# A graph attention layer on one core: block 0's bins taken inside the last merge, block 1's spread by TensorE, the sort ended at stretches of four

## The chip, the cores and the metric

The kernel runs on one core of a Trainium2 chip. The metric is device time in microseconds (us). Engines are named as the profile names them: PE is TensorE (PEld its weight loads), DVE is VectorE, ACT is ScalarE, POOL is GpSimd, and SP is the engine that only issues DMAs. PSUM is the memory that PE writes and DVE and ACT read; a line such as L514 is a line of the kernel before.

## What is computed

A graph has 4096 nodes with 64 features and 50,000 directed edges, drawn at random. For each of 4 heads, the features are projected to 64 outputs, each edge gets a score from its two ends, and each node receives the mean of its sources' projections, weighted by the exponentials of the scores:

```python
x_proj[h] = x @ weight[h]
...
src_att = np.sum(x_proj[h, src_nodes] * att_src[h], axis=-1)
dst_att = np.sum(x_proj[h, dst_nodes] * att_dst[h], axis=-1)
...
edge_scores = np.where(edge_scores > 0, edge_scores, 0.2 * edge_scores)
...
output[h, dst] += np.exp(edge_scores[h, i]) * x_proj[h, src]
...
output[h, dst] /= (total + 1e-8)
```

The output is 4096 x 256 in float32.

## The kernel before

The edges have to be brought to their nodes first, and this is done by sorting.

**First sort (to 68 us).** Each of the 128 partitions holds 391 edges as numeric keys. `Sorter` is a bitonic sorting network on DVE: a step (`half(j)`, L203 to L210) compares elements 2^j apart with one minimum and one maximum. `rows` sorts each partition's row of 512; `runs` (L240) then merges eight rows into a run, in two rounds: transpose, a few steps across rows, transpose back, and the steps j = 8 down to 0 inside the rows. The runs go to memory (`gat_sorted1`). Beside it ACT counts with Sign and an accumulator how many keys of each row lie below each of 17 bounds (`below`, L265), PE adds the counts up (L282), and DVE works out where each group of 256 source nodes begins and ends in each run (`bounds`, L277 to L291: one conversion, then multiply, reduce, add for the starts `ws` and again for the ends `we`).

**Second sort (72 to 115 us).** POOL gathers, for each of 16 source groups, its share of each run (`fetch`, L308). Eight partitions make one source group now. They are merged the same way, this time by destination, and the last step writes the keys as integers (`ki`), which SP stores to memory (`gat_sorted2`, L263). ACT counts again, against 33 bounds, one for each block of 125 destination nodes, and the same `bounds` gives the start of each block in each group.

**The seam (115 to 131 us).** `Windows` (L377) has POOL gather, in 5 pieces of 8 blocks each, the 128 keys from each start on: 16 rows of 128 keys for a block, enough for all of its edges and some of its neighbours'. `unpack(i)` (L386) splits a piece into the source within the group and the destination within the block (`tb`, two halves) with four small operations on DVE, or three on DVE and one on ACT for piece 0, and stores both to memory (`gat_bins`). `Blocks.load(b)` (L414) reads them back so that every partition has all 2 x 2048 numbers of block b (`bc`, 1 MB written). For block 0 alone this is done without memory: `spread` (L421) has PE multiply `tb` with one column of the identity repeated 128 times, once per row, and ACT and DVE copy the result from PSUM. Between them stand two `longest` (L293), which find the longest stretch of the first and of the second sort (two small DVE operations, a transpose by PE, and a maximum into `most`); `room` (L303) has every engine read `most` into registers, for a test at the end of the kernel: if a stretch is longer than its window (256 and 128), a second, general pass runs. Six dense matmuls whose result nobody reads follow on PE (`warm`, L646).

**The blocks (131 to 297 us).** `Blocks.run` (L520) takes the 33 blocks in order. For a block: `onehot` (L436) compares `bc` with the partition's number and leaves 0/1 matrices `oh` (DVE, two instructions, L446 and L449); `gather(b, c)` (L452) has PE multiply them with the node tables, in three parts of 6, 6 and 4 groups, each part into one of two PSUM buffers, and ACT takes the exponentials (`ex`, L475) and copies the values (`xs`, L477); `weights` (L481) and `values` (L490) make `wv` and `val` on DVE; `sums` (L500) adds the weights up (k < 0) and the values (k = 0 and 1, L514) by PE into `acc`, which ACT copies away (`aT`, L564); `project` (L566) multiplies with the weights, and once for every two blocks `invert` and `give` (L571 to L582) divide and store.

**What sets the order.** Everything up to the test at the end stands in a stretch with a manual schedule: each engine runs its instructions in the order in which the program writes them, and waits only for data and buffers. Block b's iteration issues: `load(b+4)`, `values(b)`, `gather(b+1, 0)`, `project(b-1)`, `sums(b, -1)`, the rest of `gather(b+1)`, the first half of `onehot(b+2)`, `weights(b+1)`, the second half, `sums(b, 0)` and `(b, 1)`. An `unpack` that is handed to `run` (`also`, L545) comes last in its iteration. DMAs are issued in program order too; nearly all are SP's. `bc` has 4 buffers; `oh`, `ex`, `xs`, `wv` and `val` have 2.

Before the change, the seam is written so (L638 to L655):

```python
group(so2, pp2, ws1[:])
win = Windows(cst, ws2[:])
longest(so2, pp2, ws1, we1, 0)
longest(so2, pp2, ws2, we2, 1)
n1, n2 = room(0, EL), room(1, L)
...
win.unpack(0, nc.sync, nc.scalar)
for b in range(1, 4):
    blocks.load(b)
for i in range(1, 4):
    win.unpack(i, nc.sync, nc.sync)
blocks.spread(0, win.tb[:, 0])
blocks.run({i - 3: lambda i=i: win.unpack(i, nc.sync, nc.sync) for i in range(4, NI)})
```

Of the kernel before, what the change touches and what calls it, by code (L numbers as in the profile page):

```python
# [11 lines left out]
P = 128  # L12
ALPHA = 0.2
F32 = mybir.dt.float32
BF16 = mybir.dt.bfloat16
# [6 lines left out]
L = 512  # L22
# [5 lines left out]
BD = 125  # L28
KPAD = float(1 << 24)
# [8 lines left out]
def kernel(ctx: ExitStack, tc: tile.TileContext, x: bass.AP, edge_index: bass.AP,  # L38
# [141 lines left out]
    class Sorter:  # L180
# [59 lines left out]
        def runs(self, to=None):  # L240


            s, d = self.step()
            V.stream_shuffle(out=self.z[:], in_=s[:], mask=[p ^ 1 for p in range(32)])
            V.tensor_scalar(out=self.y[:], in0=s[:], scalar1=sig[:, 0:1], scalar2=None, op0=OP.mult)
            V.scalar_tensor_tensor(out=d[:], in0=av(self.z[:], L - 1, [-1, L]), scalar=sig[:, 0:1], in1=self.y[:],
                                   op0=OP.mult, op1=OP.min)
            s, d = self.step()
            V.tensor_scalar(out=d[:], in0=s[:], scalar1=sj[0][:, 0:1], scalar2=None, op0=OP.mult)
            for j in range(8, -1, -1):  # L250
                self.half(j)
            for m in range(1, 3):
                self.turn()
                self.opposed(m)
                for j in range(m - 1, -1, -1):
                    self.half(j)
                self.turn()
                for j in range(8, -1, -1):
                    self.half(j, to=to if m == 2 and j == 0 else None)
            return to or self.a[self.cur]  # L260
# [16 lines left out]
    def bounds(pool, pp, sgn, nt, n, sels, off, mask, nk, ws, we):  # L277

        ni = ws.shape[1] // len(sels)
        for i, sel in enumerate(sels):  # L280
            ps = pp.tile([P, nt + 1], F32, name=f"cnt_ps{i}")
            T.matmul(out=ps[:], lhsT=sel, rhs=sgn[:], start=True, stop=True)  # L282
            cnt = pool.tile([P, nt + 1], F32, name=f"cnt{i}")
# [9 lines left out]
    def longest(pool, pp, ws, we, k):  # L293

        mx = pool.tile([P, ws.shape[1]], F32, name=f"mx{k}")
        V.tensor_tensor(out=mx[:], in0=we[:], in1=ws[:], op=OP.subtract)
        mx1 = pool.tile([P, 1], F32, name=f"mxr{k}")
        V.tensor_reduce(out=mx1[:], in_=mx[:], axis=AX, op=OP.max)
        mx_ps = pp.tile([1, P], F32, name=f"mx_ps{k}")
        T.transpose(out=mx_ps[:], in_=mx1[:], identity=ident[:])  # L300
        V.tensor_reduce(out=most[:, k:k + 1], in_=mx_ps[:], axis=AX, op=OP.max)
# [15 lines left out]
    def group(pool, pp, start):  # L317
# [7 lines left out]
        so.rows(9)  # L325
        ki = pool.tile([P, L], I32, name="ki")
        store(skey2, so.runs(ki))
        bounds(pool, pp, sgn, 8 * NI, L, [sel2[:]], off2, m8, 8, ws2, we2)
# [73 lines left out]
    class Blocks:  # L402
# [18 lines left out]
        def spread(self, b, tb):  # L421

            bc = self.bc[b] = self.bcp.tile([P, 2, NT * W2], BF16, name="bc")
            for c, (t0, n) in enumerate(CH):
                ps = self.psx.tile([P, CH[0][1], PW], F32, name="ps")
                for i in range(n):
                    T.matmul(out=ps[:, i, :], lhsT=av(identb[:], b * NT + t0 + i, [0, P]), rhs=tb, start=(i % 2 == 0),
                             stop=True, skip_group_check=True)
                (S.copy if c < 2 else V.tensor_copy)(out=av(bc[:], t0 * W2, [W2, n], [NT * W2, 2], [1, W2]),
                                                     in_=av(ps[:], 0, [PW, n], [W2, 2], [1, W2]))  # L430
                if c == 1:
                    self.onehot(b, *CH[0])
            for c in (1, 2):
                self.onehot(b, *CH[c])
# [85 lines left out]
        def run(self, also={}):  # L520
# [4 lines left out]
            for b in range(ND):  # L525
# [89 lines left out]
    with tc.tile_pool(name="sort1", bufs=1) as so1, tc.tile_pool(name="pre", bufs=1) as pr, \  # L615
# [19 lines left out]
        so.rows(1, EL)  # L635
        store(skey1, so.runs())
        bounds(so1, pp1, sgn, NR, EL, [sel1[:, 0, :], sel1[:, 1, :]], off1, m16, NR, ws1, we1)
    with tc.tile_pool(name="sort2", bufs=1) as so2, tc.tile_pool(name="pp2", bufs=1, space=PSUM) as pp2:  # L638
        group(so2, pp2, ws1[:])
        win = Windows(cst, ws2[:])  # L640
        longest(so2, pp2, ws1, we1, 0)
        longest(so2, pp2, ws2, we2, 1)
        n1, n2 = room(0, EL), room(1, L)
        warm = pp2.tile([P, L], F32, name="warm")
        for i in range(6):
            T.matmul(out=warm[:], lhsT=identb[:], rhs=adb[:, 0:4, 0:P], start=True, stop=True)  # L646
    with ExitStack() as st:
        blocks = Blocks(st, Finish(st))
        win.unpack(0, nc.sync, nc.scalar)
        for b in range(1, 4):  # L650
            blocks.load(b)
        for i in range(1, 4):
            win.unpack(i, nc.sync, nc.sync)
        blocks.spread(0, win.tb[:, 0])
        blocks.run({i - 3: lambda i=i: win.unpack(i, nc.sync, nc.sync) for i in range(4, NI)})  # L655
# [3 lines left out]
    with tc.If((n1 > W1) | (n2 > W2)):  # L659
        with tc.tile_pool(name="all", bufs=1) as al:  # L660
            total = al.tile([P, ND, AW], F32)
            V.memset(total[:], 0.0)
            with tc.For_i(0, n1, W1):
                at1 = advance(al, ws1, we1, W1, 1)
                with tc.tile_pool(name="sort3", bufs=1) as so3, tc.tile_pool(name="pp3", bufs=1, space=PSUM) as pp3:
                    group(so3, pp3, at1[:])
                    longest(so3, pp3, ws2, we2, 1)
                m2 = room(1, L)
                with tc.For_i(0, m2, W2):
                    with ExitStack() as st:  # L670
# [6 lines left out]
                        blocks.onehot(0)  # L677
                        blocks.run()
# [40 lines left out]
```

## Time and profile before

| | |
|---|---|
| seven runs | median 300.23 us, 299.18 to 303.67 |
| the profiled execution | 299.06 us, of which the span from first to last instruction is 297.2 |
| busy: PE, DVE, ACT | 200.5 us (67%), 261.2 us (88%), 181.5 us (61%) |
| granted PE clock, mean | 0.855 |
| first sort's store issued | 68.17 |
| second sort's store issued | 114.85 |
| end of the waits for ACT's counts on PE | 105.80 |
| 136 to 284 us | PE busy 146.02 of 148.00, DVE 140.69, ACT 116.02 |

The page of a profile gives, among other things, the busy share of each engine in 40 equal slices (one digit a slice, in tenths; 9 is 90% or more), with the clock that TensorE was granted in the row PEclk. The timeline gives instructions with start and duration in us from the start of the span, and, in brackets, how long the engine sat idle before and what it was waiting for. The waits give, for each pair of waiting and releasing instruction, the us in total, how often, and the longest. Starts of one engine's instructions can lie closer together than their durations, since they overlap in its pipeline; what an instruction costs its engine is then read from start to start.

### The profile page before, as it was taken

Reading aid. Unit: us, or ns where it says so; the run is one execution under the profiler, and the core shown is the slowest. Engines: PE = TensorE matmul, PEld = TensorE weight load, DVE = VectorE, ACT = ScalarE, POOL = GpSimd, SP = SyncE. Lnnn points to the kernel's source line nnn. Section 1 sums busy time; section 2 is a strip of 40 time slices with the busy share of each in tenths; the row PEclk is TensorE's granted clock in tenths of the full one; section 3 lists DMA queues with packets and bytes.
Section 4 is the critical chain, followed back from the end, with each engine's and each line's share of the span. In section 5 each row is a group of like instructions: output and inputs, shape, how many; then the busy total and the mean of one; then the engine's idle time right before and its main releaser. Section 6 shows DMA issues by size and latency. Waiting matters only on the chain.

```text
span 297.2 us, 8429 instructions
## 1 busy us (share of the span) xinstructions
PE 200.5 (67%) x3531; PEld 191.1 (64%) x3531; DVE 261.2 (88%) x495; ACT 181.5 (61%) x355; POOL 27.2 (9%) x78
## 2 busy tenths in 40 slices
PE   0001999950000001769999999999999999999990
PEld 0000699950000000459999999999999999999980
DVE  5999999994699997689999999999999999999960
ACT  2950710050699920477787778777787878777840
POOL 7882000002000001500000000000000000000000
PEclk9999975555555555799999999999999999999997
DMA  3025000001000000497678666875587567854012
GB/s 108 1 57 103 0 2 0 0 1 42 30 0 0 0 0 35 110 385 295 202 273 295 213 206 249 303 249 204 216 306 267 197 210 292 286 195 187 10 39 59
DMA packets 13358, 41.80 MB, mean 141 GB/s; under 512 B 3120, under 2 KB 8816, under 8 KB 9216
## 3 DMA queue, kind: packets, MB, share of 16 engines
q1 hardware_dynamic: 10776, 38.97, 36.2%
q10 hardware_dynamic: 1832, 1.55, 2.2%
q0 software_dynamic: 704, 0.66, 1.1%
q8 instruction: 30, 0.49, 0.7%
q14 instruction: 16, 0.13, 0.1%
HBM read 36.13 MB, written 5.05 MB: 139 GB/s over the span
## 4 chain that ended last, share of the span: by engine, by line
PE 54%; DVE 36%; DMA 4%; issue 3%; POOL 0%; ACT 0%; DVEq 0%; POOLq 0%; SPq 0%
PE acc L514 20%; DVE sA L209 13%; DVE sB L209 12%; PE ps L469 10%; PE pf L568 7%; PE ps L467 6%; PE ps L473 5%; PE acc L509 5%; DMA bc<-gat_bins 2%; DVE sB L238 1%; DMA eS<-in_edge_index_dram 1%; DMA raw<-gat_sorted,wi 1%; PE warm L646 1%; DVE sA L198 1%; DVE val L495 1%
## 5 line engine op out<-in xcount | busy, mean ns | idle before, releaser
L477 ACT CAST xs<-ps 128x1200 bf16<-128x1200 f32 (+1 forms) x99 | 104.1, 1051 | 0.0
L495 DVE TENSOR_TENSOR val<-xs,wv 128x4096 bf16<-128x4096 bf16 (+1 forms) x34 | 75.4, 2221 | 0.6 <-ACT xs L477 0.5
L514 PE MATMUL acc<-xs,val 128*128 128x125 bf16 x1056 | 63.6, 218 | 0.2
L469 PE MATMUL ps<-adb,oh 128*128 128x136 bf16 x528 | 61.4, 223 | 0.0
L467 PE MATMUL ps<-xa,oh 128*128 128x72 bf16 x528 | 58.8, 196 | 3.4 <-DVE oh L446 2.5
L514 PEld LDWEIGHTS <-val 128*128 128x128 bf16 x1056 | 58.8, 98 | 0.5 <-DVE val L495 0.4
L469 PEld LDWEIGHTS <-oh 128*128 128x128 bf16 x528 | 49.0, 98 | 0.4 <-issue 0.3
L467 PEld LDWEIGHTS <-oh 128*128 128x128 bf16 x528 | 46.9, 98 | 3.5 <-DVE oh L446 3.5
L475 ACT ACTIVATE ex<-ps 128x96 bf16<-128x96 f32 (+1 forms) x99 | 25.0, 252 | 31.2 <-PE ps L473 31.2
L446 DVE TENSOR_SCALAR oh<-bc,pF 128x4096 bf16<-128x4096 bf16 (+2 forms) x35 | 42.0, 1201 | 0.8 <-DMA bc<-gat_bins 0.8
L209 DVE TENSOR_TENSOR sA<-sB 128x256 f32<-128x256 f32 (+2 forms) x106 | 38.0, 400 | 1.8
L209 DVE TENSOR_TENSOR sB<-sA 128x256 f32<-128x256 f32 (+2 forms) x100 | 35.9, 400 | 1.7
L473 PE MATMUL ps<-xa,oh 128*128 128x72 bf16 x528 | 33.3, 198 | 0.0
L282 PE MATMUL cnt_ps<-sgn,sel 128*128 128x17 f32 (+1 forms) x6 | 1.7, 390 | 42.1 <-ACT sgn L274 42.1
L282 PEld LDWEIGHTS cnt_ps<-sgn,sel 128*128 128x128 f32 x6 | 1.4, 318 | 42.2 <-issue 42.2
L473 PEld LDWEIGHTS <-oh 128*128 128x128 bf16 x528 | 26.3, 99 | 0.1
L367 PEld LDWEIGHTS at_ps<-uv,xT 64*128 64x128 f32 x130 | 25.2, 302 | 0.2 <-issue 0.2
L367 PE MATMUL at_ps<-uv,xT 64*128 64x4 f32 x130 | 25.3, 331 | 0.0
L449 DVE TENSOR_SCALAR oh<-bc,pF 128x2048 bf16<-128x2048 bf16 (+2 forms) x35 | 25.1, 717 | 0.0
L568 PE MATMUL pf<-Wbd,aT 128*128 128x128 f32 x132 | 22.7, 295 | 2.9 <-ACT aT L564 0.9
L271 ACT ACTIVATE junk<-kr,nb 128x512 f32<-128x512 f32 x33 | 23.8, 722 | 1.1
L568 PEld LDWEIGHTS pf<-Wbd,aT 128*128 128x128 f32 x132 | 17.3, 191 | 4.7 <-issue 3.4
(130 smaller groups left out, 203.2 us busy)
## 6 DMA issues: line engine op xcount, KB each, us to landing
bc<-gat_bins SPq DMA_DIRECT2D x32, 1024.0 KB, 9.0
out_dram<-res SPq DMA_DIRECT2D x32, 125.0 KB
eS<-in_edge_index_dram SPq DMA_DIRECT2D x2, 195.0 KB
eD<-in_edge_index_dram ACTq DMA_DIRECT2D x2, 195.0 KB
gat_bins<-tb SPq DMA_DIRECT2D x9, 32.0 KB
gat_sorted<-sA SPq DMA_DIRECT2D x1, 256.0 KB
gat_sorted<-ki SPq DMA_DIRECT2D x1, 256.0 KB
out_dram<-res SPq DMA_DIRECT2D x1, 96.0 KB
```

The costliest lines, as they stand in the source:

```text
L209: V.tensor_tensor(out=av(d[:], o, [2 * h, n], [1, h]), in0=av(s[:], 0, [2 * h, n], [1, h]), in1=av(s[:], h, [2 * h, n], [1, h]), op=op)
L367: T.matmul(out=ps[:, b, :], lhsT=xT[:, b * step:b * step + P], rhs=uv[:, k, :], start=(b == 0), stop=True, skip_group_check=True)
L446: V.tensor_scalar(out=oh[:, 0:2, e], in0=bc[:, :, e], scalar1=pF[:, 0:1], scalar2=None, op0=OP.is_equal)
L449: V.tensor_scalar(out=oh[:, 2, e], in0=bc[:, 1, e], scalar1=pF[:, 1:2], scalar2=None, op0=OP.is_equal)
L467: T.matmul(out=ps[:, i, P:P + XC], lhsT=oh[:, 1, e], rhs=xa[:, 2 * t, :], start=(i % 2 == 0), stop=False, skip_group_check=True)
L469: T.matmul(out=ps[:, i, 0:S0], lhsT=oh[:, 0, e], rhs=adb[:, b, :], start=False, stop=False, skip_group_check=True)
L473: T.matmul(out=ps[:, i, P:P + XC], lhsT=oh[:, 2, t * W2:(t + 1) * W2], rhs=xa[:, 2 * t + 1, :], start=False, stop=True, skip_group_check=True)
L475: S.activation(out=av(ex[:], 2 * t0, [2, n], [2 * NT, 2 * H], [1, 2]), in_=av(ps[:], P, [PW, n], [1, 2 * H], [0, 2]), func=ACTF.Exp)
L477: S.copy(out=xs[:, t0:t0 + n, 0:P + XC], in_=ps[:, 0:n, 0:P + XC])
L495: V.tensor_tensor(out=av(val[:], h * Dout, [Dout, n], [C, NT], [1, Din]), in0=av(xs[:], S0, [0, n], [XW, NT], [1, Din]), in1=av(wv[:], h * ...
L514: T.matmul(out=self.acc[:, k * BD:(k + 1) * BD], lhsT=val[:, t, k * P:(k + 1) * P], rhs=xs[:, t, 0:BD], start=False, stop=(t == NT - 1), s ...
L568: T.matmul(out=self.pf[:, b % 2, k * P:(k + 1) * P], lhsT=self.aT[:, b % 2, k * BD:k * BD + P], rhs=Wbd[:, k, :], start=(b % 2 == 0 and k ...
```

## The change

- **The sort's end.** In the second sort, the last merge stops after the step j = 2 (`FINE = 2`): the keys then stand in stretches of four, each stretch right as a whole and its four in any order. That step writes `ki` now. The starts `ws2` are rounded down and the ends `we2` up to multiples of four (`whole`, three operations each), so that a window still takes in all of a block's keys.
- **Block 0's bins.** After the merge's step j = 7 the first 128 keys of a group already stand in the first 128 columns of its first row. There a hook, `spy`, makes them relative to the group on DVE (`kb0`), and one step later splits them (`t0`); ACT casts them (`tb0`), and PE spreads them over the partitions, row 8t for group t, with the copies from PSUM all on ACT. Block 0 no longer needs the store, the gather or `unpack(0)`.
- **Block 1.** It is spread by PE from `unpack(0)`'s `tb`, as block 0 was; loads from memory begin with block 2. Its copies are two on ACT and one on DVE.
- **Order.** The one-hots and the gather of block 0 come right after the bounds. `unpack(0)` follows them, with both stores on SP, then the loads of blocks 2 to 4, `weights(0)`, `values(0)`, the spread of block 1, and block 0's sums between the parts of block 1's gather. `unpack(1)`, the two `longest` (with one maximum for both) and the reading of `most` into registers stand before `sums(0, 1)`. `unpack` 2, 3 and 4 stand in the iterations of blocks 1, 2 and 3.
- **The rest.** The six `warm` matmuls are gone. The counting matmul (`counts`) is issued before the merge instead of after it, and its PSUM buffer and that of `longest` are lent by the block stage, whose buffers now exist during the second sort.

```diff
-        def runs(self, to=None):
+        def runs(self, to=None, fine=0, spy=None):
...
-                for j in range(8, -1, -1):
-                    self.half(j, to=to if m == 2 and j == 0 else None)
+                last = fine if m == 2 else 0
+                todo = []
+                for j in range(8, last - 1, -1):
+                    self.half(j, to=to if m == 2 and j == last else None)
+                    if todo:
+                        todo.pop(0)()
+                    if m == 2 and 1 << j == W2 and spy:
+                        todo = spy(self.a[self.cur])
...
+    def whole(pool, t, up, what):
+        i = pool.tile([P, NI], I32, name=f"whole{what}")
+        V.tensor_scalar(out=i[:], in0=t[:], scalar1=float(up), scalar2=None, op0=OP.add)
+        V.tensor_scalar(out=i[:], in0=i[:], scalar1=FINE, scalar2=FINE, op0=OP.logical_shift_right,
+                        op1=OP.logical_shift_left)
+        V.tensor_copy(out=t[:], in_=i[:])
...
-        store(skey2, so.runs(ki))
-        bounds(pool, pp, sgn, 8 * NI, L, [sel2[:]], off2, m8, 8, ws2, we2)
+        cps = counts(pool, pp, sgn, 8 * NI, [sel2[:]])
+        store(skey2, so.runs(ki, FINE, spy))
+        bounds(pool, cps, 8 * NI, L, off2, m8, 8, ws2, we2)
+        whole(pool, ws2, 0, 0)
...
-        def spread(self, b, tb):
+        def spread(self, b, c, tb, row, copy):
+            if c == 0:
+                self.bc[b] = self.bcp.tile([P, 2, NT * W2], BF16, name="bc")
+            t0, n = CH[c]
+            ps = self.psx.tile([P, CH[0][1], PW], F32, name="ps")
+            for i in range(n):
+                T.matmul(out=ps[:, i, :], lhsT=av(identb[:], row(t0 + i), [0, P]), rhs=tb, start=(i % 2 == 0),
+                         stop=True, skip_group_check=True)
+            copy(out=av(self.bc[b][:], t0 * W2, [W2, n], [NT * W2, 2], [1, W2]),
+                 in_=av(ps[:], 0, [PW, n], [W2, 2], [1, W2]))
...
+        def spy(keys):
+            def relative():
+                V.tensor_scalar(out=kb0[:], in0=keys[:, 0:W2], scalar1=goff[:, 0:1], scalar2=None, op0=OP.add)
+            def split():
+                V.tensor_scalar(out=t0[:, 0, :], in0=kb0[:], scalar1=8, scalar2=None, op0=OP.logical_shift_right)
+                V.tensor_scalar(out=t0[:, 1, :], in0=kb0[:], scalar1=SG - 1, scalar2=None, op0=OP.bitwise_and)
+                S.copy(out=tb0[:], in_=t0[:])
+                for c in range(len(CH)):
+                    blocks.spread(0, c, tb0[:], lambda t: RUN * t, S.copy)
+            relative()
+            return [split]
+        group(so2, Lent(), ws1[:], spy)
         win = Windows(cst, ws2[:])
-        longest(so2, pp2, ws1, we1, 0)
-        longest(so2, pp2, ws2, we2, 1)
+        whole(so2, we2, (1 << FINE) - 1, 1)
+        for c in range(len(CH)):
+            blocks.onehot(0, *CH[c])
+            blocks.gather(0, c)
+        win.unpack(0, nc.sync, nc.sync)
+        for b in range(2, 5):
+            blocks.load(b)
+        blocks.weights(0)
+        blocks.values(0)
+        for c in range(len(CH)):
+            blocks.spread(1, c, win.tb[:, 0], lambda t: NT + t, S.copy if c < 2 else V.tensor_copy)
+            if c == 1:
+                blocks.onehot(1, *CH[0])
+        for c in (1, 2):
+            blocks.onehot(1, *CH[c])
+        blocks.sums(0, -1)
+        blocks.gather(1, 0)
+        blocks.sums(0, 0)
+        blocks.gather(1, 1)
+        blocks.gather(1, 2)
+        win.unpack(1, nc.sync, nc.sync)
+        longest(so2, Lent(), (ws1, we1), (ws2, we2))
         n1, n2 = room(0, EL), room(1, L)
-        warm = pp2.tile([P, L], F32, name="warm")
-        for i in range(6):
-            T.matmul(out=warm[:], lhsT=identb[:], rhs=adb[:, 0:4, 0:P], start=True, stop=True)
...
-        blocks.spread(0, win.tb[:, 0])
-        blocks.run({i - 3: lambda i=i: win.unpack(i, nc.sync, nc.sync) for i in range(4, NI)})
+        blocks.sums(0, 1)
+        blocks.weights(1)
+        blocks.onehot(2)
+        blocks.run(1, {i - 1: lambda i=i: win.unpack(i, nc.sync, nc.sync) for i in range(2, NI)})
```

## The prediction

> **What bounds the kernel now.** I read the page's slices first, then the timeline of the stretch where the second sort hands over to the blocks, and last the waits inside the block loop.
>
> ```profile
> PE   0001999950000001769999999999999999999990
> DVE  5999999994699997689999999999999999999960
> PEclk9999975555555555799999999999999999999997
> ```
>
> Each digit is 7.43 us. VectorE (DVE) is full up to slice 15: the two sorts, which end at 114.7. From slice 18 on (133.7) TensorE (PE) is full. Between them lies a seam of some 16 us in which no engine is full, and TensorE enters it at half clock. The change works on this seam. Its timeline (start, duration, engine, line, operation; in brackets the idle time before and what ended it):
>
> ```profile
> 113.89 0.76 DVE L209 TENSOR_TENSOR ki<-sB 128x256 int32<-128x256 f32 x2
> ...
> 115.89 0.16 DVE L312 CAST wi<-ws 128x5 int32<-128x5 f32 x1
> ...
> 117.58 0.94 POOL L314 DMA_INDIRECT win<-gat_sorted,wi  x1 [42.76 <-DVE mxr L298]
> ...
> 120.17 0.23 DVE L388 TENSOR_SCALAR t<-win 128x128 int32<-128x128 int32 x1 [2.12 <-DMA win<-gat_sorted,wi]
> ...
> 123.28 1.28 SPq L417 DMA_DIRECT2D bc<-gat_bins  x3
> ...
> 128.90 1.29 DVE L446 TENSOR_SCALAR oh<-bc,pF 128x4096 bf16<-128x4096 bf16 x1 [0.77 <-DMA bc<-gat_bins]
> ...
> 131.08 2.29 DVE L495 TENSOR_TENSOR val<-xs,wv 128x4096 bf16<-128x4096 bf16 x1
> ```
>
> The sorted keys go to memory (issued 114.85), the windows come back from 117.58 on, the bins go out and block 1's come back at 128.87. The first `val` (block 0) starts at 131.08. After that, the waits of 136 to 284 us show TensorE waiting for almost nothing, and DVE for little:
>
> ```profile
> ACT ex L475 <- PE ps L473: 28.7, 62, 0.7
> DVE wv L487 <- ACT ex L475: 5.6, 15, 0.6
> PEld pf L568 <- issue: 3.4, 15, 0.2
> ...
> PEld L514 <- DVE val L495: 0.2, 1, 0.2
> ```
>
> A pair of blocks takes 9.72 us (152.91 to 162.62), and DVE's `val` ends only 0.1 to 0.5 us before TensorE's sums (L514) want it: 143.0 against 143.07, 147.87 against 148.03, 152.28 against 152.74. So the end moves by what the seam saves, less what DVE is given to do in the loop beyond 0.37 us a pair (5.6 / 15).
>
> **The change, part by part.** I lay the new order of each engine end to end with the durations above; DVE's clock starts from `half(7)` of the last merge, 108.32 as before.
>
> *Sort end.* Steps of the merge start 0.80 apart (112.30, 113.09, 113.89); two fall away: -1.59. Three operations on 128 columns come in (`kb0`, two for `t0`); L388 and L389 stand 0.13 to 0.14 apart: +0.42 taken, 0.3 to 1.1 as ends (1.1 if each costs L392's 0.28 to 0.50). The counts start at about 113.5 instead of 114.57.
>
> *Rounding.* The bounds take 1.32 to the place of `wi`, as now (114.57 to 115.89). Each `whole` adds three dependent operations on 128x5; dependent small ones stand 0.20 to 0.24 apart (114.80, 115.03, 115.27). With `wi` I take 1.25, ends 0.9 and 1.45. Block 0's first one-hot can start at 113.5 + 1.32 + 1.25 = 116.1; before it was 124.53.
>
> *Block 0's bins under the sort.* ScalarE (ACT) has been idle since 105.7. Cast 0.4 (0.30 for half as much); 16 matmuls of 256 columns at half clock 0.213 each (the warm-up's 512 columns stood 0.43 apart); copies 1.34 apart, the last 1.05. The three parts of `bc` are there at 113.7, 115.1 and 116.0; DVE wants them at 116.1, 117.0 and 117.8. Hidden by the end of the sort, with 1.8 us to spare; beyond that each us late is a us on the path.
>
> *gather(0).* TensorE starts 0.65 after the one-hot, 116.75. A part takes 0.75 (the last 0.5) at full clock. At half clock, 1.4, 1.4 and 0.95; ACT behind it (ex and xs 1.2 a part) is done at 122.1, and `val(0)` starts at **122.2**, 8.9 earlier than 131.08. At full clock it is 121.1.
>
> *Block 1 spread by TensorE: here most of that is given back.* The window lands at 119.1 (the store is issued 1.1 earlier, and 2.6 us lie from gather to landing) and DVE splits it by 119.7, but the cast of `tb` (L391, on ACT) is queued behind the six ACT instructions of gather(0): it ends at 122.4. The 16 matmuls, the second store to `gat_bins` and all loads behind it on SP wait for it. ACT copies to 124.6 and 125.8. DVE, the one that ends last, has in its queue: `val(0)` 2.2, to 124.4; one-hot 0.86 from 124.7; copy 1.13 (125.39 to 126.52); one-hots 0.86 and 0.71, to 128.2; `unpack(1)` 0.62, to 128.85; the four small operations of `longest` 0.46; transpose and maximum 0.4 and 0.6, to 130.3. Then it must read `most` into registers:
>
> ```profile
> L305 PEldq TENSOR_LOAD <-most x2: 311/402/492, 117.4 to 118.1; - x2
> L305 DVEq TENSOR_LOAD <-most x2: 321/434/548, 117.8 to 118.4; - x2
> ```
>
> Before, this lay under the wait for the window. Now `weights(1)` and `onehot(2)` are queued behind it on DVE, and `sums(0,1)` and gather(2) on TensorE. From `most` (118.06) to the end of DVE's second load (118.4 + 0.32) it is 0.66: free at 130.95. (For comparison only: the Trainium skill, "DMA: Bandwidth & Descriptors", section "Latency and other measured facts", gives one such load a floor of about 0.6 us. These loads took 0.32 and 0.55, so the row decides; two at 0.6 would take about half a us off the saving.) Then `wv` 0.14, and `onehot(2)` starts at 131.1, gather(2) at 132.4 (before: 135.20), `val(1)` at 132.9 (135.28), the sums of block 1 at 135.5 (138.15): **2.65 earlier**.
>
> Block 2's bins: last store issued at 122.45, loads 2.18 later (121.10 to 123.28), first landing 5.59 after that: 130.2, under DVE's 131.1 by 0.9.
>
> *In the loop.* `unpack` 2, 3 and 4 now stand in iterations 1, 2 and 3, where before only 4 stood, in iteration 1. That is 2 x 0.6 = 1.2 us more on DVE (140.13 to 140.73), `val` being behind it. DVE's waits for `ex` (0.37 a pair) and its lead of 0.46 at block 4 take up about half; 0.65 comes through. Block 4's sums: 150.7 instead of 152.74.
>
> **Sum: 2.65 - 0.65 = 2.0 us earlier.** Against the profiled execution, 299.06 (span 297.2 and 1.86 around it), that is 297.1. The seven times have the median 300.23, so I forecast **298.2**.
>
> **What the clock does** is the largest unknown. The six warm-up matmuls are gone. In the trace TensorE fell to half clock at 40.7 while its row was 100% busy with 4-column matmuls, and came back at 122.26 (0.74 in the stretch 122.0 to 122.5), 3.8 us after the first warm-up matmul. Counted 3.8 us from gather(0)'s start, the clock is back at 120.5: that is the case above. Back already through the 16 spread matmuls (by 116.7), the sum gives 3.1; back only during block 1 (121 to 128), 1.1 to 1.3.
>
> The Trainium skill, "TensorE: Matmul & The Clock Gate", section "What's actually happening", has a rule against deleting the warm-up: the gate counts free-running windows of 3.4 us, a busy one frees the clock, an idle one takes it. The trace's 3.8 us fits one such window. By the rule the spread's 3.6 us can fill a window only if it begins just right, which points to the middle case and not to 3.1.
>
> **Rivals.**
> (A) *The spread warms TensorE*, 3.1 us: 297.1. For it, 16 dense matmuls in 3.6 us; against it, the gap for the PSUM copy and 2.1 idle us after.
> (B) *The clock is late*, back in block 1, 1.2 us: 299.0. For it, gather(0) at half clock waits for ACT's buffers.
> (C) *Block 2's bins come late.* The page's median from issue to landing of a `bc` load is 9.0; then they land at 133.6, 2.5 after DVE wants them, and the time is 300.7: no change. Against it, the first of three loads landed in 5.59. It costs from 6.5 on.
> (D) *Slower: the clock stays at half into the loop.* Its place is gather(1) to the sums of block 2; TensorE needs twice its 4.9 us a block. Laid out so, the saving is 0 with the clock back at 130, and at 136 the kernel is 1.2 slower: 301.4, with 0.3 more for each further us. For it, 40.7 shows that a busy row is not enough; against it, these very matmuls hold the clock at 1.00 from 122.5 on with 50% gaps.
> (E) *The change spoils the windows*: rounding widens them, and one over 128 keys would send the kernel into its second pass, as much again as 71 to 297. Counted on the reference's draw, the widest is 124: not taken.
>
> **Chances.** Forecast 0.39, A 0.22, B 0.18, C 0.10, D 0.10, E 0.01. A measurement of this kernel can tell about 0.3%, 0.9 us, from no change. The forecast's own bounds (1.0 below, 0.8 above by the ends of the small costs) leave it mostly faster, B partly, C on the line, D slower: faster 0.69, within 0.18, slower 0.13. The range: A with the low ends gives 296.3; upward it takes in B and C and leaves out D: 300.7.
>
> **What would show it.** Right: the first `val` near 122; `cast tb` waiting behind `xs` on ACT; gather(2) near 132.4; DVE idle about 1 us around the register loads; TensorE waiting for `val` in iterations 2 and 3; clock at 1.00 from about 120.5. Wrong: `val(0)` later than 123.5 (small operations dearer), `onehot(2)` released by the DMA (C), half clock after 126 (D), or `unpack` without effect on block 4's sums (then 0.6 more is saved).

## The result and the profile after

The changed kernel takes **298.38 us** (median of 31 runs, 296.85 to 301.38); the kernel before took 300.2 (73 runs, 298.77 to 303.95). The ratio is 0.9938, with a 95% interval of 0.9922 to 0.9954: 1.8 us by the medians, where 2.0 were forecast.

The profiled execution of the changed kernel took 300.25 us (span 298.3), 1.9 more than its median; that of the kernel before took 299.06, 1.1 less than its median. Side by side, these two would show a loss, so the first thing to learn is how far one execution stands from the median. The slices of the changed kernel, from its page:

```profile
PE   0001999950000027769999999999999999999980
DVE  5999999994799998678999999999999999999950
PEclk9999975555555555588999999999999999999996
```

A slice is 7.46 us now. Counted from 0, TensorE does more in slices 14 and 15 (the spread and block 0's gather have come forward), yet the row of the clock comes back from 5 one slice later, and only to 8. The timeline of the seam (start, duration, engine, line, operation; in brackets the idle time before and what ended it):

```profile
112.47 0.76 DVE L210 TENSOR_TENSOR ki<-sB 128x256 int32<-128x256 f32 x2
...
116.15 1.08 POOL L340 DMA_INDIRECT win<-gat_sorted,wi  x1 [41.31 <-DVE we L316]
...
118.79 0.23 DVE L416 TENSOR_SCALAR t<-win 128x128 int32<-128x128 int32 x1 [0.69 <-DMA win<-gat_sorted,wi]
...
121.34 0.33 ACT L419 CAST tb<-t 128x128 bf16<-128x128 int32 x1
...
121.51 2.29 DVE L520 TENSOR_TENSOR val<-xs,wv 128x4096 bf16<-128x4096 bf16 x1 [0.49 <-ACT xs L502]
121.72 2.72 PE L456 MATMUL ps<-tb,identb 128*128 128x256 bf16 x12 [1.35 <-ACT tb L419]
...
124.72 0.62 DVE L471 TENSOR_SCALAR oh<-bc,pF 128x1536 bf16<-128x1536 bf16 x1 [0.92 <-ACT bc L458]
...
131.80 0.23 DVE L512 TENSOR_TENSOR wv<-ex 128x128 bf16<-128x128 bf16 x1 [1.37 <-ACT xs L502]
...
133.80 2.29 DVE L520 TENSOR_TENSOR val<-xs,wv 128x4096 bf16<-128x4096 bf16 x1
```

The order is the one laid out: the first `val` 9.6 us earlier than 131.08, the cast of `tb` on ACT behind block 0's `xs`, TensorE waiting for it, DVE waiting 0.92 for the copy. Then almost everything is given back: the second `val` comes at 133.80, against 135.28. In the loop, over the same 136 to 284 us as before, the waits stay small, and TensorE now waits a little for `val` (twice, 0.6 us in all):

```profile
ACT ex L500 <- PE ps L498: 28.8, 61, 0.9
DVE wv L512 <- ACT ex L500: 5.9, 14, 1.3
...
PEld L539 <- DVE val L520: 0.6, 2, 0.5
```

The new wait of the change stands ahead of the loop, in the waits of the whole execution. It is TensorE's stop of 1.8 us at the register loads, ahead of `sums(0, 1)`:

```profile
PE acc L539 <- issue: 1.8, 1, 1.8
```

### The profile page after: what moved, and what is told of

Read it like the earlier page. It is cut to its first block, busy times and chain, and to the rows that moved or that the text cites. A ratio compares the mean times of both kernels' runs of the same rounds, so it can differ in the third digit from the quotient of the medians.

```text
span 298.3 us, 8448 instructions
## 1 busy us (share of the span) xinstructions
PE 205.7 (69%) x3541; PEld 196.3 (66%) x3541; DVE 260.9 (87%) x503; ACT 185.7 (62%) x359; POOL 27.5 (9%) x78
## 4 chain that ended last, share of the span: by engine, by line
PE 50%; DVE 39%; issue 3%; DMA 2%; ACT 2%; DVEq 0%; POOL 0%; POOLq 0%; ACTq 0%
PE acc L539 18%; DVE sA L210 13%; DVE sB L210 12%; PE ps L494 10%; PE pf L595 6%; PE ps L492 6%; PE ps L498 5%; PE acc L534 4%; DVE val L520 2%; DVE sB L239 1%; DVE oh L471 1%; DMA eS<-in_edge_index_dram 1%; ACT xs L502 1%; DMA raw<-gat_sorted,wi 1%; PE ps L456 1%
## 5 line engine op out<-in xcount | busy, mean ns | idle before, releaser
L494 PE MATMUL ps<-adb,oh 128*128 128x136 bf16 x528 | 63.1, 226 | 0.0
L492 PE MATMUL ps<-xa,oh 128*128 128x72 bf16 x528 | 60.3, 199 | 2.0 <-DVE oh L471 2.0
L494 PEld LDWEIGHTS <-oh 128*128 128x128 bf16 x528 | 50.1, 100 | 0.1
L492 PEld LDWEIGHTS <-oh 128*128 128x128 bf16 x528 | 47.8, 99 | 2.7 <-DVE oh L471 2.7
L210 DVE TENSOR_TENSOR sA<-sB 128x256 f32<-128x256 f32 (+2 forms) x104 | 37.3, 400 | 1.8
L210 DVE TENSOR_TENSOR sB<-sA 128x256 f32<-128x256 f32 (+2 forms) x98 | 35.1, 400 | 1.6
L498 PE MATMUL ps<-xa,oh 128*128 128x72 bf16 x528 | 34.1, 200 | 0.0
L498 PEld LDWEIGHTS <-oh 128*128 128x128 bf16 x528 | 27.1, 100 | 0.0
```

The source lines that it names most:

```text
L210: V.tensor_tensor(out=av(d[:], o, [2 * h, n], [1, h]), in0=av(s[:], 0, [2 * h, n], [1, h]), in1=av(s[:], h, [2 * h, n], [1, h]), op=op)
L492: T.matmul(out=ps[:, i, P:P + XC], lhsT=oh[:, 1, e], rhs=xa[:, 2 * t, :], start=(i % 2 == 0), stop=False, skip_group_check=True)
L494: T.matmul(out=ps[:, i, 0:S0], lhsT=oh[:, 0, e], rhs=adb[:, b, :], start=False, stop=False, skip_group_check=True)
L498: T.matmul(out=ps[:, i, P:P + XC], lhsT=oh[:, 2, t * W2:(t + 1) * W2], rhs=xa[:, 2 * t + 1, :], start=False, stop=True, skip_group_check=True)
```

## The experiments

Each kernel was timed against the kernel before on its own chip. Medians of the kernel before there were 299.8 to 300.2, so a ratio is safer to compare than a time. Differences under 0.3% (0.9 us) are read from the traces, if at all.

### The changed kernel once more

No edit; a second trace.

> The changed kernel once more, unedited, for a second trace beside its times. My theory: the saving is made at the seam and is about 2 us; the first trace (298.3) is a late one because the clock fell back to half at 132.47 for one window of 3.41 us after TensorE had idled 1.75 us at the register loads. A trace in which the clock does not fall back should have a span near 296.3 and block 4's val near 148.5 (first trace 150.23). Rival: the first trace is typical, the saving of the times lies behind the last instruction, and the second trace again shows block 4's val at 150.2 whatever the clock does.

298.31 us (12 runs), ratio 0.9942 (0.9909 to 0.9976). Its profiled execution took 297.63. The two executions of one kernel, beside the forecast and the kernel before (us from the start of the span; "sums" is the start of a block's value sums on TensorE):

| | before | forecast | first | second |
|---|---|---|---|---|
| first one-hot of block 0 | 124.53 | 116.1 | 115.64 | 115.58 |
| val(0) | 131.08 | 122.2 | 121.51 | 121.01 |
| `most` done | 118.06 | 130.3 | 130.43 | 129.09 |
| onehot(2) | 133.29 | 131.1 | 131.94 | 130.31 |
| val(1) | 135.28 | 132.9 | 133.80 | 132.17 |
| sums of block 1 | 138.15 | 135.5 | 137.39 | 134.72 |
| sums of block 4 | 152.74 | 150.7 | 152.57 | 149.90 |
| DVE's last instruction ends | 291.09 | | 290.88 | 288.20 |

Block 4's `val` starts at 147.56 in the second, against 150.23 in the first, so the rival falls. Up to the end of the sort the two agree within 0.1. What differs then is mostly the clock. Both were cut at the moments at which their clock could change; the columns are the stretch, its length, TensorE's busy us with its instructions, the granted clock, the DMA share, and GB/s. First execution:

```profile
122.23:125.64 3.41, 3.11 (x17) 0.50 0.29 69
125.64:129.06 3.42, 3.42 (x82) 1.00 1.00 419
129.06:132.47 3.41, 1.32 (x18) 1.00 1.03 423
132.47:135.88 3.41, 3.07 (x35) 0.50 0.96 363
```

Second execution:

```profile
109.96:113.37 3.41, 2.72 (x12) 0.50 0.00 0
113.37:116.79 3.42, 1.13 (x16) 1.00 0.21 79
116.79:120.20 3.41, 3.08 (x41) 0.50 0.16 43
120.20:123.61 3.41, 1.47 (x12) 1.00 0.24 58
...
127.03:130.44 3.41, 1.84 (x33) 1.00 1.01 269
```

In every trace of this case the clock changes at moments that are whole multiples of 3.413 us apart, and where these fall against the program differs from execution to execution. A busy stretch is followed by full clock (122.23 in the first execution, 109.96 and 116.79 in the second), a thin one by half, though the one from 120.20 on kept full clock with 1.47 us busy. In the second execution the spread of block 0 filled a stretch and brought full clock for the next one (113.37 to 116.79); after that block 0's gather filled a stretch at half clock, and the clock was back from 120.2 on. In the first it came at 125.64, and behind the stretch with the stop at the register loads (1.32 us busy) it was gone again for the gather of block 2: DVE waited 1.28 us for that gather's `ex` (at 138.56), against 0.24 in the second execution (at 135.89). In the second execution the same stop fell across two stretches, with 1.84 and 2.89 us busy, and nothing was lost. Among the runs of the changed kernel, those with a mean clock of 0.86 or more took 296.9 to 298.2 us, those with 0.846 or less 299.3 to 301.4.

The Trainium skill, "TensorE: Matmul & The Clock Gate", section "What's actually happening", calls the window free-running, 3413 ns long, and says that this shifts the transition from run to run. The traces agree, and add a number. Block 1's sums lie 2.7 us apart (137.39 and 134.72): 0.5 of it arose up to `val(0)`, 0.8 more up to `most`, 0.3 in the register loads, which took longer in the first execution, and 1.0 behind `val(1)`, where the clock had fallen back. So some 2.4 us go with the phase.

### The maximum and its register loads behind the loop

```diff
-        longest(so2, Lent(), (ws1, we1), (ws2, we2))
-        n1, n2 = room(0, EL), room(1, L)
...
         blocks.run(1, ...)
+        longest(so2, Lent(), (ws1, we1), (ws2, we2))
+        n1, n2 = room(0, EL), room(1, L)
```

> The changed kernel with the two longest and the register loads moved behind the block loop. My theory: they hold DVE from 129.04 to 131.80 and TensorE for 1.75 us; without them weights(1) waits for ex of block 1 only (130.07), so onehot(2) starts 1.7 us earlier, and the fall-back of the clock is rarer: 1.5 to 2.5 us faster than the changed kernel, about 296.4. Rival, the bins of block 2 come late from memory and hide the loads: 0 to 0.3 us. Rival, the loads only move to the end and cost the same there: 0.

298.1 us, ratio 0.9936 (0.9905 to 0.9967). `val(1)` starts at 131.25, 0.92 before the second execution above, and the blocks keep that. What the stop costs there is seen at `wv`, which needs block 1's last `ex`; the second execution first, then this one:

```profile
130.16 0.23 DVE L512 TENSOR_TENSOR wv<-ex 128x128 bf16<-128x128 bf16 x1 [1.07 <-ACT xs L502]
...
129.25 0.23 DVE L512 TENSOR_TENSOR wv<-ex 128x128 bf16<-128x128 bf16 x1 [1.19 <-ACT ex L500]
```

That `ex` ended at 128.95 in the second execution, 1.2 us ahead of `wv`, and at 129.21 here, right ahead of it. Then the maximum ends at 288.59 and the loads at 289.58, where TensorE's branch at the program's end starts at 289.96 instead of 287.30. So the price of the stop is 1.2 us where it stood, of which 0.9 show, since this execution's `ex` came 0.26 later. At the end more than half of that is paid again: the span is 295.3, against 295.7. The rival is nearer.

### The cast of the first window on DVE

```diff
-            (S.copy if i == 0 else V.tensor_copy)(out=tb[:, 1, :], in_=t[:, 1, :])
+            V.tensor_copy(out=tb[:, 1, :], in_=t[:, 1, :])
```

> The changed kernel with unpack(0)'s cast on DVE instead of ACT. My theory: the cast is done by 119.7 instead of 121.7, the 16 matmuls of block 1's spread run behind gather(0) from about 120.2, ACT copies from 121.5 instead of 123.25, and the one-hot of block 1 follows val(0) without the 0.9 us gap: 0.9 to 1.2 us faster than the changed kernel, about 297.4; bins to memory 1.9 us earlier too. Rival, DVE or the register loads end last anyway and the copies are covered: under 0.3 us.

297.68 us (10 runs), ratio 0.9916 (0.9883 to 0.9949): 0.6 under the changed kernel by the medians, with overlapping intervals. The cast ends at 119.1, but the spread starts at 120.47, released by `xs`: the PSUM buffer comes free no sooner. The queue on ACT that the prediction named is real, but a second wait stands close behind it: taking it away moves the spread by 0.75 us (120.47 against 121.22 in the second execution) and no further. DVE no longer waits for the copy, yet `val(1)` comes at 132.23, no earlier than the 132.17 of the second execution: `val(0)` was 0.3 later (121.30), and the register loads took 1.23 instead of 1.07. No gain at the blocks is shown.

### Dummy matmuls against the half clock

```diff
+        def warm(n):
+            ps = blocks.psx.tile([P, CH[0][1], PW], F32, name="ps")
+            for i in range(n):
+                T.matmul(out=ps[:, 0:2, :], lhsT=identb[:], rhs=adb[:, 0:4, 0:P], start=True, stop=True)
```

with `warm(9)` ahead of block 0's spread and behind it, and `warm(6)` ahead of the register loads.

> The changed kernel with dead dense matmuls on TensorE: 9 before the spread of block 0, 9 after it, 6 at the register loads. My theory of the clock: full clock for gather(0) and no fall-back at 132; gather(0)'s parts come 0.7 instead of 1.4 apart, ACT sets the pace, val(0) 0.4 to 0.9 earlier, block 1's spread 0.9 shorter: 1.0 to 2.0 us faster than the changed kernel, about 297, and with less spread among its times. Rival, the clock at the seam is covered by ACT and DVE: within 0.4 us.

298.04 us, ratio 0.9925 (0.9896 to 0.9953). The clock was full from 110.3, yet fell for 120.5 to 124.0, since block 0's gather fills only 1.64 us of the stretch before; the mean clock rose to 0.860 to 0.876. `val(1)` came at 132.74, 0.6 later than in the second execution without dummies. Half of that stands already at block 1's first one-hot (123.89 against 123.60), since the half clock fell on block 1's spread; the other half is between `wv` and `onehot(2)`, which waited 0.18 for block 2's bins, the only such wait over 0.03 in the traces of the changed kernel and its variants. Holding the clock, as far as it was held, was worth 0.3, inside the uncertainty and what the rival says.

### The sort to its end, the rest of the change kept

`FINE = 0`, and no `whole`.

> The changed kernel with the sort going down to stretches of one again and without the rounding of the bounds; the bins on the chip and the spread by TensorE stay. Theory (the sort end is worth little: two merge steps of 0.80 saved, 1.25 us of rounding paid back): block 0's val starts 0.2 to 0.5 us later than in the changed kernel (121.5), the time is 298.4 + 0.3 = 298.7. Rival (the sort end is what gains, since the store and the second block's window come 1.6 us earlier): val of block 1 is 1.0 us or more later, the time 299.4 or more. Second rival (the rounding costs more than the steps it saves): the time is 298.1 or less.

298.93 us, ratio 0.9964 (0.9928 to 0.9999), 0.55 over the changed kernel. `val(0)` is at 122.69, 0.7 later than the latest that the theory allows: the gather is issued 1.6 later (117.78), the window lands 2.9 later, and DVE stands 3.06 us at `t<-win`, ahead of block 0's `wv`. The mechanism is that of the first rival, the size nearer to the theory's.

### The three unpackings apart

```diff
-        blocks.run(1, {i - 1: ... for i in range(2, NI)})
+        blocks.run(1, {6 * i - 9: ... for i in range(2, NI)})
```

> The changed kernel with the unpacking of groups 2, 3 and 4 in iterations 3, 9 and 15 instead of 1, 2 and 3. Theory (two more unpackings of 0.6 us stand in the loop where DVE has no slack; 0.65 of the 1.2 comes through): block 4's val starts 0.5 to 0.7 us earlier counted from block 1's, the time is 298.4 - 0.6 = 297.8. Rival (an unpacking is hidden wherever it stands, or costs its 0.6 at any place since DVE's slack of 0.37 us a pair never gathers): no change, 298.2 to 298.5.

298.24 us (10 runs), ratio 0.9939 (0.9911 to 0.9967): the median shows nothing. The trace does. From the sums of block 1 to those of block 4 it is 14.63 us (136.94 to 151.57), against 15.18 in both executions of the changed kernel and 14.59 before. So the two added unpackings cost 0.59 there, and the edit takes 0.55 of it away; at the places where they went, each costs 0.15, so that 0.2 is left: from block 1's sums to the last block's it is 149.69, against 149.88.

### The kernel before with the sort's new end alone

Stretches of four, and `whole` for starts and ends; nothing else.

> The kernel before with one part of the change alone: the sort ends at stretches of four and the bounds are rounded. Theory (in the kernel before the second block's path runs store, window, bins; the store comes 1.6 us earlier and the rounding of 1.25 lies beside it): block 0's val starts 1.2 to 1.6 us earlier than 131.08, the time is 299.8 - 1.4 = 298.4. Rival (the rounding is in the way of the gather, so that only 0.3 is left): 299.5. Second rival (something behind the last instruction takes it back, as it took 1.0 to 1.4 us in the changed kernel): val 1.4 earlier, and the time 299.3 or more.

298.34 us, ratio 0.996 (0.9929 to 0.9991). From its timeline, block 0's window and `val`:

```profile
118.49 0.23 DVE L399 TENSOR_SCALAR t<-win 128x128 int32<-128x128 int32 x1 [1.02 <-DMA win<-gat_sorted,wi]
...
129.44 2.29 DVE L506 TENSOR_TENSOR val<-xs,wv 128x4096 bf16<-128x4096 bf16 x1 [0.21 <-ACT xs L488]
```

Both are 1.6 to 1.7 earlier than before (120.17, 131.08), and all sums up to block 4's and DVE's last instruction stay 1.64 earlier, as the theory has it. By itself this small part gives 1.2 to 1.8 us (by the ratio and by the medians); the rest of the change (the sort to its end, above) gives 1.1 to 1.2; together they give 1.8 to 1.9. Whether the parts add is not shown: their sum, 2.3 to 3.0, is not clear of the whole by these intervals. Nor can this small part be told from the whole change by its time (0.996 and 0.9938, with overlapping intervals).

### The kernel before without its warm-up

The six matmuls are left out.

> The kernel before without its six warm-up matmuls, nothing else. Theory (the warm-up was worth one window of the clock): TensorE is at half clock until 125.6 or 129.1, gather(0) takes 0.65 us more a part, the time is 299.8 + 0.5 to 1.5 = 300.8. Rival (ACT and the transfers pace block 0, not TensorE): val(0) within 0.3 of 131.08, no change, 299.8. The stretch from DVE's last instruction to the end of the span should be 6.1 us as in the kernel before; if it is 7 or more, that stretch is no property of the changed kernel.

299.92 us, ratio 0.9998 (0.9976 to 1.002): no difference to be seen, although the clock came back at 130.2 instead of 122.3 and `val(0)` was 0.8 later in its trace. By the time the rival holds; its sign, `val(0)` within 0.3, does not, in an execution that was itself 2.0 above its median (301.94). From DVE's last instruction to the end of the span it is 7.6 us here and 8.1 with the sort's new end alone, against 6.1 in the trace of before and 7.5 in the changed kernel; so this tail is no cost of the change.

### The reading of the windows moved forward

Where the loop's front has no cover for the stop, block 0's has. First: the four small operations behind block 0's first one-hots, the transposes between the first and second part of its gather, the loads ahead of `weights(0)`.

```diff
             blocks.onehot(0, *CH[c])
+            if c == 0:
+                mx = widest(so2, (ws1, we1), (ws2, we2))
             blocks.gather(0, c)
+            if c == 0:
+                ps = turned(Lent(), mx)
+        V.tensor_reduce(out=most[:, 0:2], in_=ps[:], axis=AX, op=OP.max)
         win.unpack(0, nc.sync, nc.sync)
...
+        n1, n2 = room(0, EL), room(1, L)
         blocks.weights(0)
...
-        longest(so2, Lent(), (ws1, we1), (ws2, we2))
-        n1, n2 = room(0, EL), room(1, L)
         blocks.sums(0, 1)
```

(`widest` and `turned` are the two halves of `longest`.)

> The changed kernel with the maximum of the windows computed between block 0's one-hots and the register loads placed ahead of block 0's weights, on every engine. Theory (the maximum and the loads cost about 0.9 us where the change put them, since DVE and TensorE have nothing else there; ahead of block 0's weights DVE waits 0.7 to 1.2 us for ACT anyway): val(1) comes 0.6 to 0.9 us earlier counted from val(0), val(0) itself within 0.3 of 121.0 to 121.5, the time is 298.4 - 0.7 = 297.7. Rival (ACT's own loads of about 0.7 us delay the copies of block 1's bins, so that the loss is only moved): onehot(1) waits for ACT's copy 0.5 us longer, and the time is 298.2 to 298.4. Second rival (the time is set by the clock and by TensorE's branch at the end, and not by what DVE saves here): no change of the median although val(1) to val(5) are earlier.

The second kernel has the loads behind the second copy of block 1's bins.

> The same, with the register loads placed after the second copy of block 1's bins and ahead of block 1's first one-hot. Theory: ACT's loads are then hidden (it waits 1 us for TensorE after that copy), DVE's fall into its wait of 0.3 to 0.9 us for the copy: 0.3 to 0.5 of the 0.7 are left on DVE, val(1) comes 0.5 to 0.9 us earlier counted from val(0), the time is 297.7. Rival (DVE's loads come on top): 298.2. If this one is faster than the placing ahead of the weights by 0.3 or more, ACT's loads are what costs there.

301.46 us (ratio 1.0058, 1.0024 to 1.0093) and 301.57 (1.0066, 1.0035 to 1.0097): slower than both kernels, and neither theory nor rival foresaw it. From the timeline of the first of the two:

```profile
123.65 0.25 ACT L518 ACTIVATE ex<-ps 128x96 bf16<-128x96 f32 x1 [4.09 <-remote]
...
125.11 0.23 DVE L530 TENSOR_TENSOR wv<-ex 128x128 bf16<-128x128 bf16 x1 [5.52 <-ACT ex L518]
```

ACT stands 4.09 us, in both kernels the same, for a semaphore of TensorE (the view writes `remote` where it finds no instruction that ended at the release). By the trace's matmul records the second part of the gather ended at 119.77; its semaphore came at 123.62. In the ten traces so far, no semaphore of a matmul was more than 0.2 late.

### The transposes behind the gather

As the second of the two, with the small operations under DVE's wait for the window, the transposes behind the gather's three parts, and the maximum between `wv` and `val`:

```diff
             blocks.gather(0, c)
+        ps = turned(Lent(), widest(so2, (ws1, we1), (ws2, we2)))
         win.unpack(0, nc.sync, nc.sync)
...
         blocks.weights(0)
+        V.tensor_reduce(out=most[:, 0:2], in_=ps[:], axis=AX, op=OP.max)
         blocks.values(0)
...
             if c == 1:
+                n1, n2 = room(0, EL), room(1, L)
                 blocks.onehot(1, *CH[0])
```

> The changed kernel with the maximum and the register loads early again, but with the two transposes of the maximum behind all three parts of block 0's gather on TensorE, the four small operations ahead of them under DVE's wait for the window, the reduction between wv and val, and the loads behind the second copy of block 1's bins. In the last two runs the semaphore of gather(0)'s second part came 4 us after its last matmul, with the transposes between the first and the second part. Theory (the transposes between two parts of a gather held the second part's end): the 4.1 us of ACT's wait are gone, val(0) is at 121.0 to 121.8 and val(1) 0.5 to 0.9 us earlier counted from it, the time is 297.7. Rival (not the place of the transposes, but the maximum's early reading or the register loads bring the stall): some wait of 4 us stays, now on the spread of block 1, and the time is 301 or more. Second rival: no stall, but the loads on DVE come on top: 298.4.

**297.01 us** (295.4 to 297.5, 6 runs), ratio 0.9903 (0.9876 to 0.9931). This beats the kernel before by about 2.8 us and the changed one by about 1 (0.0035 of the ratio), though the two intervals against before overlap at their ends. Its timeline:

```profile
120.60 2.29 DVE L538 TENSOR_TENSOR val<-xs,wv 128x4096 bf16<-128x4096 bf16 x1 [0.17 <-ACT xs L520]
...
123.55 0.62 DVE L489 TENSOR_SCALAR oh<-bc,pF 128x1536 bf16<-128x1536 bf16 x1 [0.66 <-ACT bc L476]
...
128.93 0.23 DVE L530 TENSOR_TENSOR wv<-ex 128x128 bf16<-128x128 bf16 x1 [0.98 <-ACT ex L518]
...
130.93 2.28 DVE L538 TENSOR_TENSOR val<-xs,wv 128x4096 bf16<-128x4096 bf16 x1
```

From `val(0)` to `val(1)` it is 10.33 us, against 11.16 in the second execution of the changed kernel: 0.83 less. The two executions differ in their clocks, so that is no price of the stop alone. The maximum lies in the 0.47 in which `val(0)` waited for `xs` (0.17 now), and DVE's loads run beside `val(0)`:

```profile
L349 DVEq TENSOR_LOAD <-most x2: 320/443/566, 120.6 to 121.3; - x2
```

`val(0)` is busy from 120.60 to 122.89. With `most` ready before it (120.43), the loads cost DVE nothing that shows. In the second execution of the changed kernel `most` was DVE's last result (129.09), the loads ran from 129.13 to 130.08 with nothing beside them, and `wv` came at 130.16.

### The same with the cast on DVE and the unpackings apart

The edits of both earlier sections on top.

> The last kernel (297.01) with the first window's cast on DVE and the unpacking of groups 2, 3 and 4 in iterations 3, 9 and 15. Theory (the gains add: 0.6 us from the cast, 0.2 to 0.6 from the unpacking): spread(1) starts 0.4 us earlier after block 0's last xs, val(1) 0.3 to 0.6 us earlier, block 4's val another 0.5, the time is 296.2. Rival (TensorE's PSUM buffers come free with ACT's xs anyway and DVE's loads now stand in the wait that the cast left): nothing from the cast, 296.7 to 297.0.

299.37 us, ratio 0.9967 (0.9943 to 0.9991): slower than without them by 2.4 (1.9 by the ratios). The stop is back, with the transposes behind the gather. Its ACT rows:

```profile
121.78 0.25 ACT L518 ACTIVATE ex<-ps 128x96 bf16<-128x96 f32 x1 [2.37 <-PE mx_ps L344]
...
124.01 0.23 ACT L518 ACTIVATE ex<-ps 128x64 bf16<-128x64 f32 x1 [0.93 <-remote]
```

The semaphore of the gather's second part came at 121.76 (matmul records: 119.48), that of the third at 123.99. So the transposes between two parts are not the cause, or not alone. It belongs to the program and not to one execution: the fastest of this kernel's 12 runs took 298.35, the slowest of the 6 without the two edits 297.5. What holds TensorE's semaphores there stays open. The traces show a 16 KB transfer of instructions starting at 119.1 to 119.2 in the three kernels that stopped, but at 117.5 to 119.4 in the changed kernel and its variants that did not, so it does not tell them apart.

## Why the prediction was right, step by step

- **The forecast of 298.2 against 298.38.** The mechanism is the one told: block 0 comes 9 to 10 us earlier, and block 1's spread behind ACT, DVE's full queue and the register loads give most of it back. That the size fits so well is partly luck: the terms missed to both sides, at block 4 by 0.8 us one way in one execution and by 1.9 the other way in the other, and the median lies between.
- **Sort end, rounding, first one-hot.** Forecast 116.1, measured 115.6: the added operations stood nearer to the low ends. What the sort's end alone gives at the blocks, 1.64 us, was in the forecast only as an earlier start of the counts and of the store (1.1; the store came 1.43 earlier, at 113.42).
- **val(0) at 122.2.** 0.7 to 1.2 too late in the forecast, 0.5 of it from the first one-hot. With TensorE at half clock it was 121.5, with full clock for the first half us of block 0's gather (to 116.79) 121.0.
- **The register loads, 0.66 from `most` to a free DVE.** This is the term that was mis-sized most. It measured 1.37 in the first execution and 1.07 in the second:

```profile
L331 DVEq TENSOR_LOAD <-most x2: 475/581/687, 130.5 to 131.2; - x2
L331 PEldq TENSOR_LOAD <-most x2: 532/553/574, 130.5 to 131.1; - x2
```

  In the kernel before the first load ran beside the second maximum, and the forecast read the pair from that row. Here both come behind the one maximum, one after the other: 0.69 and 0.48 us in the first execution, 0.55 and 0.32 in the second.
- **The loop, 0.65.** 0.59 from block 1's to block 4's sums, in both executions, with the two waits for `val` that were named as a sign.
- **Block 2's bins (rival C).** Not late: 131.94 was free of a DMA's wait.
- **The clock.** "Back at 120.5" is one of several courses. The second execution was that case (120.2), with a first return inside the spread, as rival A had it, and 2.84 us earlier at block 4. The first was rival B (125.64) with a relapse that nobody named, and 0.17 earlier at block 4. The forecast's 2.04 lies between them, as the median does. Of rival D only the place was right: the half clock came back in the gather of block 2, and left after 3.4 us. That the phase of the clock can move the blocks by as much as the whole forecast is shown by the two executions; how often each course comes is not. (The fall that the prediction puts at 40.7 was at 40.33: the stretch 40 to 41 has a mean of 0.67. Nothing rests on the difference.)
- **From the blocks to the end.** The forecast carried the blocks' gain to the time unchanged. From the second execution's blocks (2.89 earlier at DVE's last instruction) to its span (1.5 shorter) 1.4 us are lost, but against a trace of before with a short tail (6.1; in the traces of this case it is 5.9 to 8.1).

## What to carry to other kernels

Where an engine's clock is granted by windows of time, cost a seam with gaps as a spread over phases and not as one course, and read a change of under 1% from several executions. A stop for register loads comes from the value that they wait for: with the value ready and a long instruction running, they cost DVE nothing that shows, and behind the last block more than half of what was saved was paid again. Measure each part of a change alone before the gain is put down to the largest: here the smallest part can't be told from the whole.

## What the hardware showed

- **Thin windows and the clock.** In twelve traces, between 105 and 141 us, stretches of 3.413 us at full clock with 0.6 to 1.6 us of TensorE's busy time were followed by half clock, those with 1.5 to 3.4 kept it; at half clock, 2.7 to 3.4 us busy brought it back, and stretches up to 2.8 did not. Busy time alone doesn't separate them.
- **The branch at the end.** At the test for the second pass, TensorE's conditional branch takes 3.4 to 5.1 us by the trace's own record (the other engines' 0.05 to 0.07), and the span ends 1.6 to 5.2 us after it. The page's busy rows don't show it.
- **Held semaphores.** In three kernels semaphores came 2.3 to 3.9 us behind the recorded ends of their matmuls, at the same place. An edit of two lines took a kernel from 297.0 to 299.4 us, and its trace shows such a stop; the cause is open.
- **Loads beside an instruction.** DVE's sequencer read two registers at 120.61 to 121.58 while `val(0)` ran from 120.60 to 122.89.
